# Latent attention of a two-layer trunk: TensorE held to program order, and a unit's transposes and value products regrouped into four steps

## The chip, the core and the metric

One core of one Trainium2 chip runs the whole program in one launch. The metric is the device time of that launch in microseconds, the median of several runs. TensorE (PE in the rows) does matrix products and transposes, VectorE (DVE), ScalarE (ACT) and GpSimd (POOL) do elementwise work, and SyncE (SP) issues the DMA transfers. PEld is TensorE's loading of weights, which runs beside its products.

## The reference, cut to what matters

The program computes two layers of a transformer trunk for 128 context tokens and 512 latent tokens. Each layer mixes a short convolution, differential attention with 4 heads and latent attention with 8 heads, and then a SwiGLU block. The change lies in the attention:

```python
def diff_block(qb):
    sc = jnp.einsum("bhmqd,bhmkd->bhmqk", qb, k_all).astype(jnp.float32) * DIFF_SCALE
    p = jax.nn.softmax(sc, axis=-1)
    a = p[:, :, 0] - lam * p[:, :, 1]
    return jnp.einsum("bhqk,bhkd->bhqd", a.astype(v_all.dtype), v_all)
...
def mla_block(qb):
    sc = jnp.einsum("bhqd,bhkd->bhqk", qb, k_m).astype(jnp.float32) * MLA_SCALE
    p = jax.nn.softmax(sc, axis=-1)
    return jnp.einsum("bhqk,bhkd->bhqd", p.astype(v_m.dtype), v_m)
```

Latent tokens attend to 640 keys (512 latent and 128 cached ones), context tokens to 128 keys.

## The kernel before

The attention of a layer is a list of numbered steps. A step is one *score*: the products of 128 queries with 640 keys for one head (`scores`, L1194, six matmuls for a latent head), the row maximum on VectorE (`nm`, L1198), the exponential with its sum on ScalarE (L1209), the reciprocal (L1247) and the scaling on GpSimd (L1248). Scores are written to PSUM tiles `mm`, of which there are two; `mm` is also used by a few other products (below).

Steps are grouped in *units*: a pair of heads and half of the 512 queries. Four units of differential attention have 8 steps each, eight units of latent attention 4 steps each, 64 steps in all. When a unit's scores are done, its value part follows (`av_steps`), in five parts, one for each block of 128 keys: four 128x128 transposes of the probabilities into a PSUM tile `trx` (L1269; there are two), a copy of it to an SBUF tile `PT` (the helper `copy`, L273 on ScalarE and L275 on VectorE, in turn), and two products with the values (L1280), which accumulate in the one tile `ac` and write 64 partitions each. Part kt transposes block kt + 1 and multiplies block kt. `LAG` says how many steps behind the unit's last score the parts begin.

Between the steps stand small jobs, each tied to a step number by `put`: the attention of the 128 context tokens, two parts for each pair of heads (`diff_prompt` and `mla_prompt`; the second part, `prompt_out`, transposes twice (L1316, L1317), copies, and multiplies with the values (L1322)); the norm of the differential heads (`diff_norm`: L1361, a chain of small VectorE operations, L1369); loads of queries and keys (`load_pair`) and of the context tokens' queries and keys (`p32`, tile name `p` in the rows); and, in layer 0 only, products of the next modulation vectors (`ada_pe`, L449 and L456). `SIDE`, `LOADS` and `ADA_N` hold their steps. The second parts, the norms and the modulation share one PSUM tile `tr`.

A scheduler that goes through the recorded program with durations of its own decides the order on every engine; instructions of neighbouring steps are interleaved where it finds an engine free. The first steps run beside the projections that make queries, keys and values. When these are recorded, the loop at the end of `attention` runs the rest, from about step 29 to the last value part. This text calls that stretch the *tail*: 240 to 353 us in layer 0 and 1097 to 1204 us in layer 1. Behind it stands the output projection (L349 with `w_out`).

Of the kernel before, what the change touches and what calls it, by code (L numbers as in the profile page):

```python
# [2 lines left out]

# [5 lines left out]
F32 = mybir.dt.float32  # L9
# [46 lines left out]
ADV = 0  # L56
HOLD = 2
LOADS = (29, 37, 43, 52)
SIDE = ((34, 37), (37, 40, 43), (36, 40), (47, 50, 56), (44, 47), (49, 51), (51, 54), (60, 62))
ADA_N = 12  # L60
ADA_IN = 1
ADA_PE = 6
# [2 lines left out]
ADA_FF2 = 1  # L65
ADA_LAG = 3
LAG = 4
STEPS = {"dv": (1, 2, 1, 1, 1), "ckv0": (0, 1), "ckv1": (0, 2), "ac1": (0, 2), "ab1": (0, 2), "cq0": (0, 2), "cq1": (0, 1), "dk1": (0, 0), "dq1": (0, 0)}
PAT = "PPPt"
PATC = "Pc"  # L70
# [128 lines left out]
class Trunk:  # L199
# [112 lines left out]
    def soon(self, n, fn):  # L312

        if n:
            self.defer(n, fn)
        else:
            fn()

    def tick(self):
        for x in self.later:  # L320
# [853 lines left out]
    def load_pair(self, p):  # L1174

        nc = self.nc
        for h in (2 * p, 2 * p + 1):
            k = [self.t(F32R, "mk") for _ in range(2)]
            q = [self.t(F32R, "mq") for _ in range(2)]
            for part in range(2):  # L1180
                r = slice(32 * h, 32 * h + 32)
                self.move(q[part][:96, :512], self.qd[r, :, part, :].rearrange("r i c -> (r i) c"))
                self.move(k[part][:96, :], self.kd[r, :, part, :].rearrange("r i c -> (r i) c"))
            self.mq[h], self.mk[h] = q, k
        self.p32[p] = self.at.tile([96, 2, 2, 128], F32, tag="p32", name="p32", bufs=2)
        nc.sync.dma_start(self.p32[p], self.pd[64 * p:64 * p + 64].rearrange("(h r) i a c -> (r i) h a c", h=2))

    def scores(self, pairs, qc):

# [21 lines left out]

    def pt(self):
        if self.at:
            return self.at.tile([128, 512], F32, tag="PT", name="PT", bufs=3)
        return self.t(name="PTt")[:, 0:512]

    def diff_unit(self, l, p, hf):
# [40 lines left out]
            self.ys[2 + p] = self.t(name="yo")  # L1258
        return self.ys[2 + p]

    def av_steps(self, tiles, v, dst, hf):
        nc = self.nc
        hold = {}

        def tp(kt):
            p = self.tr(True)
            for i in range(2):
                for q in range(2):
                    nc.tensor.transpose(p[:, 256 * i + 128 * q:256 * i + 128 * q + 128],  # L1269
                                        tiles[i, q][:, 128 * kt:128 * kt + 128], self.ident)  # L1270
            pt = self.pt()
            self.copy(pt, p)
            hold[kt] = pt

        def av(kt):
            if kt == 0:
                hold["acc"] = self.ac()
            acc = hold["acc"]
            for i in range(2):
                nc.tensor.matmul(acc[64 * i:64 * i + 64, :256], v(kt, i), hold[kt][:, 256 * i:256 * i + 256],  # L1280
                                 start=(kt == 0), stop=(kt == 4))
            if kt == 4:
                c0 = 384 * hf
                self.copy(dst[:, c0:c0 + 256], acc[:, :256])

        def step(kt):
            if kt == 0:
                tp(0)
            if kt < 4:
                tp(kt + 1)  # L1290
            av(kt)

        return [lambda kt=kt: step(kt) for kt in range(5)]

    def soft_prompt(self, ps, n, neg=None):
# [86 lines left out]
    def plan_steps(self, l):  # L1382
# [7 lines left out]
        def put(step, *fs):  # L1390
            self.after.setdefault(step, []).extend(fs)

        def parts(g, *at):
            state = []

            def step():
                if not state:
                    state.append(g())
                next(state[0], None)
            for i in at:  # L1400
                put(i, step)

        def unit(kind, p, hf, n):
            hold = {}
            g0 = len(self.steps)

            def start():
                hold["u"] = kind(l, p, hf)

            def step(i):  # L1410
                if i == 0:
                    start()
                hold["u"][0][i]()

            def av(kt):
                if kt == 0:
                    _, tiles, v, dst = hold["u"]
                    hold["av"] = self.av_steps(tiles, v, dst, hf)
                hold["av"][kt]()
            for i in range(n):  # L1420
                self.steps.append(lambda i=i: step(i))
            for kt in range(5):
                put(g0 + n - 1 + LAG + (n * kt) // 5, lambda kt=kt: av(kt))

        for kind, p, hf in units:
            unit(kind, p, hf, 8 if kind == self.diff_unit else 4)
# [1 line left out]
            put(i, lambda g=g: self.assemble_diff(1, 2 * g, 2 * g + 2))  # L1428
        for p, i in enumerate(LOADS):
            put(i, lambda p=p: self.load_pair(p))  # L1430
        parts(lambda: self.diff_prompt(l, 0), *SIDE[0])
        parts(lambda: self.diff_norm(l, 0), *SIDE[1])
        parts(lambda: self.diff_prompt(l, 1), *SIDE[2])
        parts(lambda: self.diff_norm(l, 1), *SIDE[3])
        for p in range(4):
# [15 lines left out]
    def attention(self, l):  # L1451
# [8 lines left out]
        for (kind, j), n in zip(JOBS, JSTEPS):  # L1460
            n = n if isinstance(n, tuple) else (0, n)
# [7 lines left out]
            self.tick()  # L1469
        self.W.lo_pool = False  # L1470
        self.stage("tr")
        while self.g < len(self.steps) or self.after:
            self.step(1)
        self.split_y(6)
        self.split_y(7)
        self.stage("any")
# [237 lines left out]
```

## Time and profile before

| what | value |
|---|---|
| median of 3 runs | 1756.45 us (1756.1 to 1757.79) |
| profiled execution, its own time | 1756.95 us |
| span of the profiled execution | 1755.2 us |
| TensorE busy | 1698.5 us, 97% of the span |
| VectorE, ScalarE, GpSimd busy | 56%, 35%, 14% |
| tail of layer 0 and of layer 1 | 113 us and 107.2 us |

The profiled execution's own time is 0.5 us above the median of the runs, and its span leaves out 1.75 us around it. A busy share is an average over stages; matmuls are pipelined, so that TensorE can be called busy while it streams less than it could.

### The profile page before, as it was taken

What the parts mean: (1) busy time and instruction counts of PE and PEld (TensorE: products, weight loads), DVE (VectorE), ACT (ScalarE), POOL (GpSimd) and SP (SyncE); (2) the same over time, 40 slices, a digit from 0 to 9 for tenths busy, and PEclk for the clock granted to TensorE, in tenths of its full rate; (3) what the DMA queues carried; (4) which work ended last, traced back from release to release, by engine and by line L of the source; (5) the groups of instructions that cost most, each with busy time, mean ns of one, the idle gap of its engine ahead of it and who ended that gap; (6) DMA issues with size and microseconds to landing.
All of it is one profiled execution on the core that took longest, in us unless ns stands there. A gap on an engine that the chain in (4) does not pass through costs nothing.

```text
span 1755.2 us, 29477 instructions
## 1 busy us (share of the span) xinstructions
PE 1698.5 (97%) x11983; PEld 1589.4 (91%) x11983; DVE 975.0 (56%) x1824; ACT 614.1 (35%) x1046; POOL 247.7 (14%) x226
## 2 busy tenths in 40 slices
PE   7999989999999999999999999899999999999997
PEld 6998867698999999999999997678999999999997
DVE  3656777747466656756476668774652233232236
ACT  1334555524432122122245546553353212212221
POOL 0011113440001010101211111332200000000014
PEclk9999989999999999999999999899999999999998
DMA  9665584321355545545314634622212222222211
GB/s 323 210 208 142 169 252 139 119 89 51 94 153 151 156 126 145 174 133 146 107 52 148 217 121 157 173 76 75 73 61 77 81 72 73 73 78 78 68 53 60
DMA packets 100871, 217.38 MB, mean 124 GB/s; under 512 B 12160, under 2 KB 28928, under 8 KB 100736
## 3 DMA queue, kind: packets, MB, share of 16 engines
q1 hardware_dynamic: 100736, 215.50, 39.7%
q8 instruction: 94, 1.54, 0.4%
q14 instruction: 41, 0.34, 0.1%
HBM read 185.28 MB, written 30.18 MB: 123 GB/s over the span
## 4 chain that ended last, share of the span: by engine, by line
PE 86%; DVE 5%; ACT 3%; DMA 2%; issue 2%; POOL 0%; SPq 0%; POOLq 0%; ACTq 0%; DVEq 0%
PE mm L349 61%; PE mm L1194 4%; PE mm L372 4%; PE ac L1280 3%; PE mm L1513 3%; PE trx L1269 3%; PE mm L994 2%; PE mm L401 1%; DMA rawt<-in_w_ada 1%; ACT hv L781 1%; PE ac L476 1%; ACT wu L138 1%; DVE wu L140 1%; PE tr L449 1%; DMA mk<-kd 1%
## 5 line engine op out<-in xcount | busy, mean ns | idle before, releaser
L349 PE MATMUL mm<-h,wu 128*128 128x384 f32 (+1 forms) x4944 | 734.6, 309 | 1.8 <-ACT kp L908 1.5
L349 PEld LDWEIGHTS mm<-h,wu 128*128 128x128 f32 x4944 | 723.3, 188 | 8.7 <-issue 5.3
L138 ACT CAST wu<-stg 128x1024 fp32r<-128x1024 f32 (+2 forms) x200 | 201.5, 1011 | 686.1 <-PE mm L349 333.0
L140 DVE TENSOR_TENSOR wu<-stg,wu 128x1024 fp32r<-128x1024 f32 (+2 forms) x200 | 239.3, 1199 | 155.9 <-ACT wu L138 153.6
L349 PE MATMUL mm<-gh,wu 128*128 128x256 f32 (+1 forms) x1184 | 258.6, 309 | 0.0
L349 PEld LDWEIGHTS mm<-gh,wu 128*128 128x128 f32 x1184 | 198.7, 188 | 0.9 <-issue 0.6
L349 PE MATMUL mm<-gl,wu 128*128 128x384 f32 (+1 forms) x592 | 182.8, 309 | 0.0
L1198 DVE TENSOR_REDUCE nm<-mm 128x1 f32<-128x640 f32 x128 | 104.7, 818 | 50.4 <-PE mm L1194 49.6
L1547 DVE TENSOR_TENSOR gs<-gs,mm 128x640 f32<-128x640 f32 (+2 forms) x48 | 36.6, 763 | 154.2 <-PE mm L349 149.4
L668 DVE SCALAR_TENSOR_TENSOR x<-mm,ga,x 128x512 f32<-128x512 f32 x48 | 35.9, 749 | 145.6 <-PE mm L349 145.6
L349 PEld LDWEIGHTS mm<-gl,wu 128*128 128x128 f32 x592 | 111.4, 188 | 0.2 <-issue 0.2
L527 DVE SCALAR_TENSOR_TENSOR acc<-rawt,scT,acc 128x512 f32<-128x512 f32 x98 | 74.7, 763 | 60.4 <-DMA rawt<-in_w_ada 59.0
L372 PE MATMUL mm<-h,wu 128*128 128x384 f32 (+1 forms) x576 | 99.5, 331 | 7.4 <-ACT h L782 7.1
L372 PEld LDWEIGHTS mm<-h,wu 128*128 128x128 f32 x576 | 92.2, 205 | 12.6 <-ACT h L782 10.2
L349 PE MATMUL mm<-hi,wu 128*128 128x384 f32 (+1 forms) x400 | 89.9, 311 | 0.1
L687 POOL TENSOR_TENSOR accS<-x 128x640 f32<-128x640 f32 x4 | 9.9, 2488 | 507.3 <-DVE x L674 494.7
L1194 PE MATMUL mm<-mk,mq 96*128 96x384 f32 (+1 forms) x384 | 75.0, 336 | 5.2 <-ACT P L1209 2.4
L532 DVE SCALAR_TENSOR_TENSOR rawt<-rawt,scT 128x512 f32<-128x512 f32 x98 | 74.7, 762 | 2.1 <-POOL rawt L525 2.1
L1194 PEld LDWEIGHTS mm<-mk,mq 96*128 96x128 f32 x384 | 63.7, 200 | 12.3 <-ACT P L1209 5.2
L349 PEld LDWEIGHTS mm<-hi,wu 128*128 128x128 f32 x400 | 68.0, 188 | 2.6 <-issue 1.5
L1209 ACT ACTIVATE P<-mm,nm 128x640 f32<-128x640 f32 x56 | 44.6, 797 | 55.7 <-DVE nm L1198 45.0
L525 POOL TENSOR_SCALAR acc<-rawt,scT 128x512 f32<-128x512 f32 x14 | 9.8, 697 | 376.2 <-PE tr L542 376.1
(272 smaller groups left out, 2251.8 us busy)
## 6 DMA issues: line engine op xcount, KB each, us to landing
stg<-in_w_ff SPq DMA_DIRECT2D x104, 512.0 KB, 3.6
rawt<-in_w_ada SPq DMA_DIRECT2D x160, 256.0 KB, 3.1
stg<-in_w_in SPq DMA_DIRECT2D x30, 512.0 KB, 4.4
stg<-in_w_ff SPq DMA_DIRECT2D x32, 448.0 KB, 3.3
raw<-in_w_ada SPq DMA_DIRECT2D x32, 256.0 KB, 6.2
stg<-in_w_out SPq DMA_DIRECT2D x16, 512.0 KB, 4.4
mk<-kd SPq DMA_DIRECT2D x32, 240.0 KB, 5.8
mq<-qd SPq DMA_DIRECT2D x32, 192.0 KB, 5.4
```

What stands on the lines that cost most here:

```text
L138: nc.scalar.copy(u[:, 0, :ncol], t[:, :ncol])
L140: (nc.gpsimd if self.lo_pool else nc.vector).tensor_sub(u[:, 1, :ncol], t[:, :ncol], u[:, 0, :ncol].bitcast(F32))
L349: self.last = nc.tensor.matmul(out, w(k, pw), x(k, px), start=(k == 0 and i == 0), stop=(k == nk - 1 and i == 2)).ins
L372: self.last = nc.tensor.matmul(ps, u[:, pw, 128 * k:128 * k + 128], x(k, px)[:, c0:c1], start=(k == 0 and i == 0), stop=(k == NK - 1 and i ...
L527: nc.vector.scalar_tensor_tensor(self.acc[0], w, c[0], self.acc[0], ALU.mult, ALU.add)
L532: nc.vector.scalar_tensor_tensor(self.acc[1], w, c[1], self.acc[1], ALU.mult, ALU.add)
L1194: nc.tensor.matmul(ps[:, 128 + c0:128 + c1], q[:96, qc:qc + 128], k[:96, c0:c1], start=(i == 0), stop=(i == len(pairs) - 1))
L1198: nc.vector.tensor_reduce(nm, s, axis=AX.X, op=ALU.max, negate=True)
L1209: self.exp_end = nc.scalar.activation(P, s, AF.Exp, bias=nm, accum_out=sm).ins
L1269: nc.tensor.transpose(p[:, 256 * i + 128 * q:256 * i + 128 * q + 128], tiles[i, q][:, 128 * kt:128 * kt + 128], self.ident)
L1280: nc.tensor.matmul(acc[64 * i:64 * i + 64, :256], v(kt, i), hold[kt][:, 256 * i:256 * i + 256], start=(kt == 0), stop=(kt == 4))
L1513: self.last = self.nc.tensor.matmul(ps[:, c0:c1], u[:, pw, 128 * k:128 * k + 128], x(k, px)[:, c0:c1], start=(k == 0 and j == 0), stop=(k ...
```

## The change

Inside the tail every TensorE instruction is tied to the one recorded before it (`in_order`), so that the scheduler keeps TensorE's program order there. For the units that begin at step 24 or later (one unit of differential attention and the eight of latent attention) the value part has four parts in place of five: the transposes of blocks 0 and 1, of block 2, of blocks 3 and 4, and then all ten value products. They stand 3, 4, 5 and 6 steps behind the unit's last score. `PT` has six buffers for three, `p32` one for two; `p32` is loaded at steps of its own; and two context jobs stand some steps later.

```diff
-SIDE = ((34, 37), (37, 40, 43), (36, 40), (47, 50, 56), (44, 47), (49, 51), (51, 54), (60, 62))
+SIDE = ((34, 37), (37, 40, 43), (38, 41), (47, 50, 56), (44, 47), (49, 51), (54, 56), (60, 62))
+LAGM = 3
+NPT = 6
+P32 = (38, 45, 50, 56)
...
+    @contextmanager
+    def in_order(self):
+
+        traced, prev = self.nc.cur_bb.bb.instructions, self.pe_end
+        n = len(traced)
+        yield
+        for i in traced[n:]:
+            if i.engine == self.nc.tensor.engine:
+                if prev is not None:
+                    self.tc.add_manual_dep(i, prev.name, mybir.DependencyInfo(mybir.DependencyClass.NoSync,
+                                                                              mybir.DependencyReason.DATA))
+                prev = i
+        self.pe_end = prev
...
-        self.p32[p] = self.at.tile([96, 2, 2, 128], F32, tag="p32", name="p32", bufs=2)
-        nc.sync.dma_start(self.p32[p], self.pd[64 * p:64 * p + 64].rearrange("(h r) i a c -> (r i) h a c", h=2))
+
+    def load_p32(self, p):
+
+        self.p32[p] = self.at.tile([96, 2, 2, 128], F32, tag="p32", name="p32", bufs=1)
+        self.nc.sync.dma_start(self.p32[p], self.pd[64 * p:64 * p + 64].rearrange("(h r) i a c -> (r i) h a c", h=2))
...
-            return self.at.tile([128, 512], F32, tag="PT", name="PT", bufs=3)
+            return self.at.tile([128, 512], F32, tag="PT", name="PT", bufs=NPT)
...
+        if batch:
+            return [lambda kts=kts: [tp(kt) for kt in kts] for kts in ((0, 1), (2,), (3, 4))] + \
+                [lambda: [av(kt) for kt in range(5)]]
         return [lambda kt=kt: step(kt) for kt in range(5)]
...
+            batch = g0 >= 24
...
-            for kt in range(5):
-                put(g0 + n - 1 + LAG + (n * kt) // 5, lambda kt=kt: av(kt))
+            for kt in range(4 if batch else 5):
+                put(g0 + n - 1 + (LAGM + kt if batch else LAG + (n * kt) // 5), lambda kt=kt: av(kt))
...
+        for p, i in enumerate(P32):
+            put(i, lambda p=p: self.load_p32(p))
...
+        self.pe_end = None
         while self.g < len(self.steps) or self.after:
-            self.step(1)
+            with self.in_order():
+                self.step(1)
```

Three places show what the change makes of the engines' orders. The lines of the changed kernel are numbered anew: the scores are L1214 (before: L1194), the transposes L1291 (L1269), the value products L1302 (L1280), `prompt_out` L1341, L1342 and L1347 (L1316, L1317 and L1322), the context scores of latent heads L1371 (L1346).

First, TensorE in layer 1, in the middle of the tail. Before, the value products of each block stand by themselves between transposes and scores:

```order
L1194 MATMUL mm<-mk,mq 128x384 x3
L1194 MATMUL mm<-mk,mq 128x256 x3
L1280 MATMUL ac<-PT,vm 64x256 x2
L1269 MATMUL trx<-first,P 128x128 x2
L1269 MATMUL trx<-first,Pc 128x128 x2
L1346 MATMUL mm<-p_11931 128x128 x2
L1280 MATMUL ac<-PT,vm 64x256 x2
```

In the changed kernel the ten products of a unit stand in one row, behind a score:

```order
L1291 MATMUL trx<-first,P 128x128 x2
L1291 MATMUL trx<-first,Pc 128x128 x2
L1214 MATMUL mm<-mk,mq 128x384 x3
L1214 MATMUL mm<-mk,mq 128x256 x3
L1302 MATMUL ac<-PT,vm 64x256 x10
L1371 MATMUL mm<-p_12247 128x128 x2
L1214 MATMUL mm<-mk,mq 128x384 x3
```

Counted over the tails, runs of instructions that write 64 or 32 partitions (value products, L1322, L1369, and in layer 0 L449) go from 55 to 29 in layer 0 and from 42 to 18 in layer 1.

Second, TensorE at a `prompt_out` in layer 1. Before, other work stands between its transposes and its products:

```order
L1316 MATMUL tr<-first,PT 128x128
L1317 MATMUL tr<-first,PT 128x128
L1346 MATMUL mm<-p_12174 128x128 x2
L1280 MATMUL ac<-PT,vm 64x256 x2
L1269 MATMUL trx<-first,P 128x128 x2
L1269 MATMUL trx<-first,Pc 128x128 x2
L1322 MATMUL tr<-PT,vmp 64x128 x2
```

Now the products follow the transposes directly, and the copy that feeds them (VectorE or ScalarE) has nothing beside it on TensorE. This is so at six places in each layer:

```order
L1291 MATMUL trx<-first,P 128x128 x2
L1291 MATMUL trx<-first,Pc 128x128 x2
L1341 MATMUL tr<-first,PT 128x128
L1342 MATMUL tr<-first,PT 128x128
L1347 MATMUL tr<-PT,vmp 64x128 x2
L1214 MATMUL mm<-mk,mq 128x384 x3
```

In layer 0 the transpose of a modulation vector (L473 of the changed kernel) likewise stands directly behind the products that it takes (L466) at three places, and L466 directly behind the norm's products in the same tile `tr` (L1386) at two.

Third, VectorE in layer 1 at the second `diff_prompt`, whose product on TensorE (L1332, now L1357) takes a tile that VectorE multiplies first (L1329, now L1354). Before, the multiplication stands one score ahead of the operation that reads the product (L1300):

```order
L1309 TENSOR_SCALAR psm_11821<-psm_11821,neglam_491 128x2
L1329 TENSOR_TENSOR PT_11886<-kp32_9536,first_97 128x512
L1247 RECIPROCAL r0_11842<-sm_11840 128x1
L1198 TENSOR_REDUCE nm_11869<-mm_11862 128x1
L1336 TENSOR_TENSOR PT_11823<-PT_11823 128x2x128
L1300 TENSOR_REDUCE pm_11890<-mm_11888 128x4
```

Now it stands behind the copy of the step's second block of transposes, and so it is at all four `diff_prompt` of the program:

```order
L1218 TENSOR_REDUCE nm_11954<-mm_11947 128x1
L278 COPY PT_11974<-trx_11969 128x512
L1354 TENSOR_TENSOR PT_11978<-kp32_9536,first_97 128x512
L1267 RECIPROCAL r0_11959<-sm_11957 128x1
L1325 TENSOR_REDUCE pm_11982<-mm_11980 128x4
```

On TensorE the product that takes `PT_11978` stands directly behind the transposes into `trx_11969`.

## Rows read from the trace of the kernel before

**Rows 1.** The page: busy time by engine, and the chain that ended last.

```profile
PE 1698.5 (97%) x11983; PEld 1589.4 (91%) x11983; DVE 975.0 (56%) x1824; ACT 614.1 (35%) x1046; POOL 247.7 (14%) x226
...
PE 86%; DVE 5%; ACT 3%; DMA 2%; issue 2%; POOL 0%; SPq 0%; POOLq 0%; ACTq 0%; DVEq 0%
```

**Rows 2.** Busy time in stretches of both tails (columns in the first line).

```profile
core 0: us, PE busy (x) PEld busy (x) DVE busy (x) ACT busy (x) POOL busy (x), PEclk, DMA share, GB/s
258.00:342.00 84.00, 82.08 (x692) 59.84 (x691) 62.81 (x155) 43.16 (x95) 33.39 (x38) 1.00 0.48 139
...
1101.00:1111.00 10.00, 7.25 (x25) 6.19 (x26) 6.53 (x14) 4.75 (x10) 1.60 (x2) 0.51 1.02 317
...
1115.00:1193.00 78.00, 75.72 (x558) 56.36 (x558) 55.21 (x133) 42.16 (x94) 30.93 (x36) 1.00 0.31 87
```

**Rows 3.** TensorE's waits (total, times, longest), layers 0 and 1; two by time.

```profile
PE mm L1194 <- ACT P L1209: 4.6, 3, 2.5
...
PE tr L1316 <- DVE ada_acc L512: 0.8, 1, 0.8
PE tr L1316 <- DVE mod L457: 0.8, 1, 0.8
...
PE mm L1194 <- ACT P L1209: 5.9, 4, 1.9
...
PE mm L1194 <- DVE r L1247: 0.9, 1, 0.9
...
242.06 0.56 PE L1194 MATMUL mm<-dkp,dqp 96*128 96x384 f32 x2 [1.89 <-ACT P L1209]
...
1102.19 0.90 PE L1194 MATMUL mm<-dkp,dqp 96*128 96x384 f32 x2 [1.83 <-ACT P L1209]
```

**Rows 4.** TensorE by time at the end of layer 1's tail (start, length).

```profile
1194.32 0.65 PE L1280 MATMUL ac<-PT,vm 128*64 128x256 f32 x4
1194.90 0.44 PE L1269 MATMUL trx<-first,P 128*128 128x128 f32 x2
...
1195.49 0.65 PE L1280 MATMUL ac<-PT,vm 128*64 128x256 f32 x4
...
1199.02 0.44 PE L1269 MATMUL trx<-first,P 128*128 128x128 f32 x2
...
1200.04 1.08 PE L1280 MATMUL ac<-PT,vm 128*64 128x256 f32 x8
1201.05 0.44 PE L1269 MATMUL trx<-first,P 128*128 128x128 f32 x2
```

**Rows 5.** All engines by time: a score, and the score that waits for its tile.

```profile
1141.96 1.13 PE L1194 MATMUL mm<-mk,mq 96*128 96x384 f32 x6
...
1142.93 0.27 PE L1269 MATMUL trx<-first,P 128*128 128x128 f32 x1
...
1143.18 0.82 DVE L1198 TENSOR_REDUCE nm<-mm 128x1 f32<-128x640 f32 x1 [0.74 <-PE mm L1194]
...
1144.10 0.79 ACT L1209 ACTIVATE P<-mm,nm 128x640 f32<-128x640 f32 x1 [4.28 <-DVE nm L1198]
...
1145.04 1.14 PE L1194 MATMUL mm<-mk,mq 96*128 96x384 f32 x6 [1.17 <-ACT P L1209]
```

**Rows 6.** Durations on VectorE and ScalarE (min/median/max ns, or by time), and a load's landing.

```profile
L273 ACT COPY PT<-trx x54: 574/586/598, 256.0 to 1202.9; 128x512 f32<-128x512 f32 x54
L275 DVE COPY PT<-trx x36: 671/683/694, 257.4 to 1201.8; 128x512 f32<-128x512 f32 x36
...
313.22 0.42 DVE L275 COPY PT<-tr 128x256 f32<-128x256 f32 x1 [0.59 <-PE tr L1317]
...
L1329 DVE TENSOR_TENSOR PT<-kp,first x4: 680/849/1098, 234.3 to 1117.3; 128x512 f32<-128x512 f32 x4
...
312.35 0.28 DVE L512 TENSOR_TENSOR ada_acc<-tr,ada_acc 128x128 f32<-128x128 f32 x1
...
DMA to landing us min/median/max: 2.5/3.5/6.9
```

More of the change, by code (lines that the diff above doesn't have):

```diff
@@ L1 @@
 import math
-from contextlib import ExitStack, nullcontext
+from contextlib import ExitStack, contextmanager, nullcontext
 import numpy as np
@@ L1259, in ob, with av_steps @@
         return self.ys[2 + p]
-    def av_steps(self, tiles, v, dst, hf):
+    def av_steps(self, tiles, v, dst, hf, batch):
         nc = self.nc
@@ L1417, in av @@
                     _, tiles, v, dst = hold["u"]
-                    hold["av"] = self.av_steps(tiles, v, dst, hf)
+                    hold["av"] = self.av_steps(tiles, v, dst, hf, batch)
                 hold["av"][kt]()
```

## The prediction

> **What bounds the kernel now.** I read the page first, then the busy times of the two tails, TensorE's waits there, and its instructions by time. The page shows TensorE busy for 97% of the span, and 86% of the chain that ended last is its own work [rows 1]. In the tails it is the same: 82.1 of 84 us and 75.7 of 78 us in their long middles, while VectorE is busy for 75% and 71% of them [rows 2]. The waits outside the first 10 us of each tail are few. In layer 0 three waits for the exponential sum to 4.6 us, of which 1.89 and 2.5 lie at the start, and two for the shared tile `tr` cost 0.8 each; in layer 1 the four sum to 5.9, of which 1.9 and 1.83 lie at the start, and one of 0.9 stands beside them [rows 3]. That leaves 1.8 + 3.1 = 4.9 us of waits in both. So the old order has TensorE streaming nearly all the time, and a gain must come out of the stream itself.
>
> There is something to gain in it. Products of one block go from 1194.32 to 1194.90 and four transposes from there to 1195.49, so 0.58 and 0.59 us. Eight transposes in one go take 1.02 (1199.02 to 1200.04), 0.16 less than twice 0.59, and the products of two blocks in one go 1.01, 0.15 less than twice 0.58 [rows 4]. So each change to products that write 64 partitions and back costs 0.30 us beside the products.
>
> **The change, part by part.**
>
> *Regrouping.* The order shows 26 such visits fewer in layer 0 and 24 in layer 1: 50 x 0.30 = **-15.0 us**, all on the engine that sets the pace. If part of it hides in waits it is less; -12.5 is my bound (0.25 each). The number of products, transposes and scores stays. The Trainium skill says the same of the cause ("TensorEngine Tiling (Array Packing)", Key Properties): changing the tiling mode, not merely the tile, drains the engine; by that rule only the number of changes counts, and the sum stays -15.0. The rows agree, since a visit with twice the products pays the 0.15 once.
>
> *Program order at `prompt_out`.* Two transposes, a copy on VectorE or ScalarE, and products that need it now stand in one row, 12 times. The bare chain is 0.25 us to the engine that copies (a score's last matmul gives way at 1142.93, its VectorE reader starts at 1143.18), 0.42 for the copy, and 0.15 back (the exponential ends at 1144.89, TensorE starts at 1145.04) [rows 5, 6]: 0.82, less some 0.15 of the change of layout, which then hides: 0.65 at least. But the copy also queues behind the same step's score. Counted from that score's last matmul, the maximum runs from 0.25 to 1.07; a copy behind it ends at 1.49 and the products start at 1.64, while TensorE, with four transposes (0.44) and two more, is free at 0.66: 1.0 us. Behind ten products it is 0.75, since TensorE comes later; where the norm's VectorE work, or exponential and another copy, stand ahead of it I work out 1.4 to 1.8. Mean 1.1 less the hidden 0.1: 12 x 1.0 = **+12.0 us** (bounds 7.8 and 21.6, at 0.65 and 1.8).
>
> *Program order at `diff_prompt`.* VectorE's multiplication now stands behind the copy of the second block of transposes, and TensorE's product directly behind those transposes, four times. From the end of the transposes: 0.25, the copy 0.68, the multiplication 0.68 to 1.10, 0.15 back [rows 5, 6], so 1.75 to 2.2; I take 1.8, the lower part, because a wait for the tile `mm` (next) is partly under it: **+7.2 us** (6.8 to 8.8).
>
> *The two `mm` tiles.* A score can be written when the exponential two tiles back has been read. That chain is 2.11 us (1142.93 to 1145.04 [rows 5]). Where a context product takes the other tile after eight transposes, TensorE is back after some 1.4 us (0.11 for each transpose, and as much for each of the four passes of the context products, with a little between), so it waits 0.7; I count six such places, and two of about 0.5 at the norms, less one that the modulation fills: 4.5. They replace the 4.9 us of waits above: **-0.4 us** (bounds -4.9, if these vanish, and +4, if the other engines run later than I think).
>
> *Layer 0's modulation.* Three transposes behind their own products: 0.25 + 0.28 + 0.15 [rows 5, 6], 0.7 each. Two product groups wait until a small VectorE operation, no longer than that 0.28, has read `tr`: 0.6 each. **+3.3 us** (2 to 5).
>
> *The end of each tail.* The last unit's 20 transposes stand in one row, with two tiles: a tile is back after 0.25 + 0.59 to 0.68 + 0.15, about 1.0 us, and the other tile's four transposes fill 0.44. Three such waits of 0.55 in each tail are 3.3; the old end has its own, of which these rows say nothing: I take the middle, **+1.5 us** (0 to 3.3).
>
> *Costed at nothing.* `PT` with six buffers takes no instruction. `p32` with one buffer must wait for the product before it, but four steps lie between load and use, each with a score of 0.97 and its share of the rest, over 2 us; a load lands within 6.9 us [rows 5, 6]. Uncovered it would cost at most that, and SP's loads of later heads behind it have as many steps. The start of the tails (10 us each, at a granted clock of about half in most of it [rows 2]) has nearly the same order as before: 0, within 2 us either way.
>
> One rule speaks against the change. The Trainium skill ("TensorE: Matmul & The Clock Gate", Part 2, Step-by-step) says that matmuls stay in program order and only weight loads are pulled ahead, so that a score behind a waiting product doesn't pass it. No row here shows one that passed; could it pass, the sum would lose 12.0, 7.2 and 3.3.
>
> **Sum.** -15.0 + 12.0 + 7.2 - 0.4 + 3.3 + 1.5 = +8.6 us. The profiled execution took 1756.95, so 1765.5 for such a one; it lies 0.5 above the median, so **1765.0 us**. About 0.2%, 3.5 us, is what a measurement of this kernel can tell from no change.
>
> **Rivals.**
>
> *Faster: the waits stand in for others.* The 16 waits at the context jobs cost 19.2 us in my sum; the rest is -10.6. While TensorE waits there, VectorE and ScalarE catch up, and the scores that follow find their tiles free. If a place costs net less than 0.44 us, the kernel is faster by over 0.2%; at 0.15 it is -8.2, 1748 us. For it: VectorE and ScalarE have a quarter of the middle and more to spare [rows 2]. Against: only 4.9 us of old waits are there to be replaced. Chance 0.26.
>
> *No change.* The same places cost 0.44 to 0.88 each, near the bare chain: copies seldom queue. 1753 to 1760 us, about 1757. Against it stands the order, in which the copies follow the maximum or the exponential of their step. Chance 0.20.
>
> *The clock falls in the tails.* At the start of layer 1's tail, after waits of 1.9 and 1.83 us close together, the granted clock is 0.51 for 10 us, the lower of the levels 1.2 and 2.4 GHz; in the middles it is 1.00 [rows 2, 3]. The new waits are as long at `diff_prompt` and at the worst copies. Ten us of streaming at half the clock would cost up to 5 us more in each layer: +8.6 + 10 = 1775 us. Against it: new waits are mostly single, and the waits of 0.8 to 1.17 in the old middles left the clock at 1.00. Chance 0.10. The Trainium skill has a rule to this ("Perfetto Trace Analysis", Matmul Optimizations): the engine scales power with utilization, so matmuls should run back to back in batches. The stretch at 0.51 agrees.
>
> *The regrouping saves nothing.* If the 0.30 us were the copies' lateness and not the change of layout, the waits would come without the gain: +23.6, 1780 us. Against it: the 0.15 is the same wherever I look. Chance 0.03.
>
> **How the numbers follow.** My forecast, +3.5 to +14 us (1760 to 1771), has the remaining 0.41. Slower by over 0.2%: 0.41 + 0.10 + 0.03 = 0.54; within 0.2%: 0.20; faster: 0.26. The range of 1748 to 1777 leaves out the lower half of the faster case and most of what lies beyond the clock's.
>
> **What would show it.** In the changed profile ten products of a unit should take 5 x 0.43 + 0.3, about 2.4 us in one row, against 2.9 before. Each L1347 should stand 0.65 to 1.8 us behind L1342, with a copy from `tr` as the releaser; L1357 should wait some 1.8 us for VectorE; and scores behind L1371 some 0.7 us for the exponential. The middles would then show TensorE's busy share below today's 97%, at a granted clock of 1.00. The forecast fails if the waits at the 16 places sum to less than 10 us, or if those tails' other engines run late enough to add waits at ordinary scores, of which I counted none.

## The result, and the profile after

The changed kernel takes 1777.6 us (median of 4 runs, 1772.8 to 1783.7), the kernel before 1757.1 beside it: 1.011 times as long, interval 1.0093 to 1.0126. It is slower, as forecast, but by more than twice the forecast, and 0.6 us beyond the end of the range. Eleven more runs of it (below) lie between 1773.8 and 1780.3; the median of all 15 is 1775.8, that of 76 runs of the kernel before, taken beside the experiments, 1757.7.

The page of the changed kernel, busy time by engine and the chain that ended last:

```profile
PE 1691.5 (96%) x11983; PEld 1595.9 (90%) x11983; DVE 981.6 (55%) x1824; ACT 615.0 (35%) x1046; POOL 245.3 (14%) x226
...
PE 80%; DVE 8%; ACT 5%; DMA 4%; issue 3%; SPq 1%; POOL 0%; POOLq 0%; ACTq 0%; DVEq 0%
```

TensorE does the same number of instructions as before [rows 1], and the chain that ended last now goes through VectorE and ScalarE for 13% where it was 8%. Busy time in the stretches of both tails:

```profile
core 0: us, PE busy (x) PEld busy (x) DVE busy (x) ACT busy (x) POOL busy (x), PEclk, DMA share, GB/s
...
258.00:352.00 94.00, 80.47 (x707) 64.33 (x708) 66.41 (x158) 44.48 (x97) 31.66 (x38) 0.98 0.44 127
...
1111.00:1125.00 14.00, 10.34 (x34) 7.60 (x34) 8.68 (x19) 7.00 (x15) 2.40 (x3) 0.51 1.02 300
1125.00:1212.00 87.00, 73.68 (x565) 59.95 (x566) 61.41 (x139) 45.10 (x100) 30.54 (x37) 1.00 0.29 84
```

In the middles TensorE is busy for 86% and 85%, where it was 98% and 97% [rows 2]: it now waits. In layer 1 the stretch at the granted clock of 0.51 is 14 us long, where 10 us were shown before. Below, a tail runs from the last product of the projections ahead of it to the first product of the output projection behind it; so measured the two are 115.2 and 106.7 us long before and 124.8 and 114.5 us now. The idle time that TensorE's rows show in them (every gap over 0.15 us) sums to 16.4 us before and 39.6 us now. The waits of TensorE in the tails, layer 0 and then layer 1:

```profile
PE mm L1214 <- ACT P L1229: 5.5, 3, 1.9
PE mm L1357 <- DVE r L1267: 2.9, 2, 1.5
PE tr L1347 <- DVE PT L278: 2.7, 3, 1.1
PE tr L1347 <- ACT PT L276: 2.2, 3, 1.1
PE tr L473 <- DVE ada_acc L529: 1.9, 3, 0.9
PE mm L1214 <- DVE PT L1328: 1.1, 1, 1.1
...
PE mm L1214 <- ACT P L1229: 5.4, 4, 1.9
PE tr L1347 <- DVE PT L278: 3.1, 3, 1.4
PE mm L1357 <- DVE r L1267: 2.9, 2, 1.5
PE tr L1347 <- ACT PT L276: 2.2, 3, 1.1
...
PE mm L1214 <- DVE PT L1328: 1.4, 2, 1.1
```

The prediction named these places: `prompt_out` (L1347), `diff_prompt` (L1357), the modulation (L473) and the scores (L1214) behind context scores. Of the 5.5 and 5.4 us at L1214, though, 3.7 are two waits at the start of each tail, which the kernel before has too [rows 3]; the rest are single scores behind context scores, 1.8 in layer 0 and 1.1 and 0.6 in layer 1. What a wait at the first two looks like, by time, one place each:

```profile
299.13 0.27 PE L1342 MATMUL tr<-first,PT 128*128 128x128 f32 x1
...
299.59 0.41 DVE L278 COPY PT<-tr 128x256 f32<-128x256 f32 x1
...
300.06 0.44 PE L1347 MATMUL tr<-PT,vmp 128*64 128x128 f32 x4 [0.66 <-DVE PT L278]
```

```profile
254.67 0.69 DVE L278 COPY PT<-trx 128x512 f32<-128x512 f32 x1 [0.88 <-PE trx L1291]
...
255.28 0.68 DVE L1354 TENSOR_TENSOR PT<-kp,first 128x512 f32<-128x512 f32 x1
255.88 0.15 DVE L1267 RECIPROCAL r<-sm 128x1 f32<-128x1 f32 x1
...
256.11 0.67 PE L1357 MATMUL mm<-PT,qp 128*128 128x512 f32 x1 [1.48 <-DVE r L1267]
```

In the second the row names the reciprocal as releaser, but the operand is written by the multiplication L1354, which ends at 255.96; the product starts 0.15 later. Both places have the form that the prediction gave them; in the first pattern the wait is longest, 1.5 us, where other work of VectorE stands ahead of the copy.

A single wait is counted here as in the prediction, from the point at which TensorE could go on. For a transpose that is 0.11 us after its start, some 0.16 us earlier than the end that its row has: the wait at 300.06 above is 0.82 by this count and 0.66 by the row. Sums over a tail are the rows' own idle time.

Ten products of a unit in one row:

```profile
318.26 2.38 PE L1302 MATMUL ac<-PT,vm 128*64 128x256 f32 x20
320.56 0.45 PE L1214 MATMUL mm<-mk,mq 96*128 96x384 f32 x1
```

That is 2.30 us from their start to the next score, where the kernel before needed five times 0.58 [rows 4].

### The profile page after: what moved, and what is told of

Its sections match the earlier page's. It is cut to its first block, busy times and chain, and to the rows that moved or that the text cites. A ratio compares the mean times of both kernels' runs of the same rounds, so it can differ in the third digit from the quotient of the medians.

```text
span 1771.0 us, 29478 instructions
## 1 busy us (share of the span) xinstructions
PE 1691.5 (96%) x11983; PEld 1595.9 (90%) x11983; DVE 981.6 (55%) x1824; ACT 615.0 (35%) x1046; POOL 245.3 (14%) x226
## 3 DMA queue, kind: packets, MB, share of 16 engines
q8 instruction: 94, 1.54, 0.4%
## 4 chain that ended last, share of the span: by engine, by line
PE 80%; DVE 8%; ACT 5%; DMA 4%; issue 3%; SPq 1%; POOL 0%; POOLq 0%; ACTq 0%; DVEq 0%
PE mm L366 60%; PE mm L1214 4%; PE mm L389 3%; PE mm L1543 3%; PE ac L1302 2%; PE mm L418 2%; PE trx L1291 1%; ACT hv L798 1%; DVE nm L1218 1%; PE mm L1011 1%; PE ac L493 1%; DMA stg<-in_w_in 1%; DMA mk<-kd 1%; ACT PT L276 1%; ACT wu L141 1%
## 5 line engine op out<-in xcount | busy, mean ns | idle before, releaser
L1214 PE MATMUL mm<-mk,mq 96*128 96x384 f32 (+1 forms) x384 | 80.4, 346 | 9.0 <-ACT P L1229 3.5
L1214 PEld LDWEIGHTS mm<-mk,mq 96*128 96x128 f32 x384 | 65.7, 203 | 22.7 <-issue 11.4
L366 PE MATMUL mm<-lo,wu 128*128 128x384 f32 (+1 forms) x200 | 61.8, 309 | 0.0
```

Source lines behind the costliest of these rows:

```text
L366: self.last = nc.tensor.matmul(out, w(k, pw), x(k, px), start=(k == 0 and i == 0), stop=(k == nk - 1 and i == 2)).ins
L1214: nc.tensor.matmul(ps[:, 128 + c0:128 + c1], q[:96, qc:qc + 128], k[:96, c0:c1], start=(i == 0), stop=(i == len(pairs) - 1))
```

## The experiments

Two figures of a run help to compare kernels that differ by a few microseconds: its time, and the mean granted clock of its span (1 is full speed). Within one kernel the runs with the lower mean clock are the longer ones. Over 175 runs of the 14 kernels, each kernel taken about its own mean, 0.001 less of mean clock goes with 1.5 us more. The last column moves a kernel's mean time along this slope to a mean clock of 0.984, that of the kernel before. This is a correlation, not a cause shown. The error of a mean so moved is 0.2 to 0.9 us, so that two rows of the table differ by more than the noise only where they are some 2 us apart.

| kernel | median us (runs) | times before (95%) | mean clock | us at 0.984 |
|---|---|---|---|---|
| before | 1757.7 (76) | | 0.984 | 1758.7 |
| changed (three times) | 1775.8 (15) | 1.011, 1.010, 1.011 | 0.980 | 1771.9 |
| e1_free | 1758.3 (10) | 1.0007 (0.9997 to 1.0016) | 0.984 | 1758.2 |
| e3_out | 1771.3 (10) | 1.0071 (1.0053 to 1.0089) | 0.980 | 1766.2 |
| e4_km | 1767.6 (10) | 1.0046 (1.0020 to 1.0071) | 0.982 | 1765.3 |
| e5_waits | 1764.5 (5) | 1.0049 (1.0031 to 1.0067) | 0.979 | 1758.1 |
| e6_ring | 1783.0 (4) | 1.0148 (1.0133 to 1.0163) | 0.978 | 1774.4 |
| e7_all | 1756.3 (10) | 0.9992 (0.9983 to 1.0002) | 0.983 | 1754.9 |
| e8_visits | 1779.7 (4) | 1.0105 (1.0061 to 1.0149) | 0.981 | 1775.2 |
| e9_split | 1756.1 (10) | 0.9988 (0.9967 to 1.0010) | 0.981 | 1753.1 |
| e10_fill | 1798.2 (4) | 1.0211 (1.0177 to 1.0245) | 0.982 | 1794.4 |
| e11_late | 1748.5 (6) | 0.9939 (0.9916 to 0.9962) | 0.984 | 1748.7 |
| e12_fill | 1776.1 (6) | 1.0094 (1.0076 to 1.0112) | 0.982 | 1770.7 |
| e13_split | 1776.6 (5) | 1.0110 (1.0089 to 1.0130) | 0.980 | 1770.3 |

**Without the binding.**

```diff
-            with self.in_order():
-                self.step(1)
+            self.step(1)
```

> The change without the binding of TensorE to program order; the four-part value work, the buffers and the moved jobs stay. If the loss comes from TensorE waiting where program order puts a dependent product directly behind what it needs, the scheduler fills those places again: 1750 to 1760 us, about as fast as before (its order has 53 and 37 visits to 64 or 32 partitions, 55 and 42 before, which is worth 2 us). If the loss comes from the regrouping itself (value work later, six PT buffers, one p32 buffer), it stays above 1768 us.

1758.3 us, no different from the kernel before. The scheduler takes the regrouped value parts apart again: in the rows of the two tails TensorE goes to products that write 64 or 32 partitions 51 and 37 times, where the kernel before does 51 and 42 times by the same count and the changed one 29 and 18. So the loss comes with the binding, and so does the gain in visits. (The opposite, binding without regrouping, wasn't tried; I expect the old value parts of two neighbouring units to wait for each other there over the one tile `ac`.)

**The waits at the context jobs.** e3_out puts the products of `prompt_out` a step behind their transposes, e4_km the multiplication of `diff_prompt` a step ahead of its product, and e5_waits does both and, inside the tail, puts the end of a modulation vector a step later (last pair of lines). `SIDE` gets the extra steps:

```diff
 self.copy(pt[:, :256], p[:, :256])
-acc = p[:, 256:384]
+yield
+acc = self.tr()[:, 256:384]
...
 nc.vector.tensor_mul(kv, ...)
+yield
 ps = self.mm()
...
-self.ada_finish(self.ada_part, key)
+self.after.setdefault(self.g + 1, []).append(lambda acc=self.ada_part: self.ada_finish(acc, key))
```

> The changed kernel with the products of prompt_out one step behind their transposes and copy (12 places). Theory (the 12.2 us of waits there are net cost): the waits go, of which 2 to 3 us come back as waits for the shared tile tr, so 9 to 10 us less than the changed kernel, near 1768 where the changed kernel has 1777. Rival (a wait there lets the other engines catch up, so that it replaces others): waits at the scores behind the context jobs grow by most of it, and the time stays within 3 us of the changed kernel's.

> The changed kernel with diff_prompt's multiplication one step ahead of its product (4 places). Theory (the 6.8 us of waits there are net cost): TensorE has no wait at that product, 6 to 7 us less than the changed kernel, near 1771 where the changed kernel has 1777. Rival (part of the wait hides a wait for the tile mm behind it): 3 to 4 us come back as waits of the scores behind that product, so near 1774.

> The change, with the dependent work a step later: prompt_out's products one step behind its transposes, diff_prompt's multiplication one step ahead of its product, the modulation's transpose one step behind its products. The profile of the change shows 12.2 us, 6.9 us and 2.7 us of waits there. If these waits are lost time, 1756 to 1766 us; if they only stand in for waits that TensorE would have anyway (the two mm tiles), less than 5 us comes back, 1770 us or more.

e4_km: the theory holds. No wait at the product is left, and the time at equal clock is 6.6 us less than the changed kernel's, for waits of 6.8 (by the plain medians 8.2 us less). e3_out lies between theory and rival: 12.2 us of waits go (10.2 by the rows), 5.7 come off at equal clock. Its waits in layer 0 show where some of the rest went:

```profile
PE mm L1214 <- ACT P L1229: 6.4, 5, 1.9
PE tr L473 <- DVE ada_acc L529: 1.9, 3, 0.9
PE mm L1214 <- DVE PT L1328: 1.6, 1, 1.6
PE mm L1358 <- DVE r L1267: 1.5, 1, 1.5
PE mm L1358 <- DVE PT L1355: 0.9, 1, 0.9
PE tr L466 <- ACT yo L276: 0.8, 2, 0.4
```

The scores wait 8.0 where it was 6.6, and the modulation now waits for the copy out of `tr` (L466, twice by this row). In both tails the rows' waits fall from 39.6 to 31.2 us, by less than the 10.2 taken away. So a wait at `prompt_out` did stand in for others, by about half if one goes by time and by less if one goes by the rows. All three edits together (e5_waits) bring 13.8 us at equal clock, and the rows' waits are 25.1.

**The tiles of the context scores.** e6_ring writes the scores of `diff_prompt` and `mla_prompt` into `tr`, so that they leave the two `mm` tiles to the others; e7_all does this on top of e5_waits, e9_split does it in layer 1 alone, and e11_late in layer 0 too for the last two latent pairs, the third of the four pairs a step later, behind the modulation. The lines are e11_late's; e6_ring has `self.tr()` without a condition:

```diff
-ps = self.mm()
+ps = self.tr() if l or p >= 2 else self.mm()
...
-... (54, 56, 57), (60, 62, 63))
+... (55, 57, 58), (60, 62, 63))
```

> The change, with the context tokens' scores written to the tile tr in place of an mm tile, so that the latent scores alternate between two mm tiles undisturbed. The profile of the change shows about 8 us of waits of scores behind L1371 and some 1.5 us behind L1357. If the mm tiles are the part of the loss that the prediction priced too low, 1763 to 1771 us; if those waits come from late VectorE and ScalarE in general, within 3 us of the change.

> Both repairs together: dependent work a step later, and context scores in tr. If regrouping saves what its fewer changes of layout promise (about 10 us by the profile of the change, 15 by the prediction) and the waits are the whole loss, this is faster than the kernel before: 1744 to 1754 us. If it ends at 1757 us or above, the regrouped order has costs of its own.

> All three waits taken away as in e7_all, but the context scores take the tile tr in layer 1 alone, and mm in layer 0, where the modulation's products use tr as well. Theory (places add up, and each tail is what it was in the run that had it best): tails of 116.9 and 101.6 us as profiled, against 122.5 and 101.6 in e7_all, so 5.6 less than e7_all's 1756.3: 1751 us, and faster than the kernel before by 0.3%. Rival (the tails' length is set by time at the lower granted clock, which comes and goes with the order): 1756 or more, with low-clock time in layer 0's tail as in e7_all.

> e9_split with two places of layer 0 moved: the context scores of the last two latent pairs take tr there too, and those of the third pair stand a step later, behind the last modulation products. e9_split shows waits of 2.65 and 1.73 us at the scores behind these two places, and 5 of 0.5 to 0.7 at the modulation that stay. Theory: these 4 us go from layer 0's tail (117.1 to about 113.5) and nothing comes in their place, so 3 to 4 us below e9_split's 1756: 1752 to 1753, faster than the kernel before by 0.3%. Rival (time at the lower clock eats it, as it did with e7_all's 5.5 us): span times mean clock falls from 1722.5 to 1719, but the time stays at 1755 or above.

e6_ring was a miss: slower still. In layer 0 `tr` now makes the modulation wait, in three rows of its waits there:

```profile
PE tr L466 <- issue: 2.6, 2, 1.6
...
PE tr L466 <- DVE dv L1388: 1.8, 2, 1.5
PE tr L466 <- DVE PT L1328: 1.6, 1, 1.6
```

In layer 1, without modulation, the scores' waits behind context scores went from 3.3 us to 0.4, and its tail from 114.5 us to 112.4, with 20.5 us at the lower clock in it where the changed kernel's trace has 13.7. e7_all, with e5_waits under it, is as fast as the kernel before; its tail of layer 1 is 101.6 us long, that of layer 0 still 122.5. e9_split takes the good half: its profiled tails are 117.1 and 102.0 us long, as the theory had it (116.9 and 101.6), yet its median equals e7_all's, at a mean clock of 0.981 against 0.983; the rival was right about the time. At equal clock it is 1.8 better, not 5.6. The two profiled runs show where it went: their mean clocks are the same (0.982), the tails are 5.0 us shorter in sum, but the span only 1.4. Outside the tails the lower clock was granted for 20.4 us, in e7_all's run for 13.6. e11_late is as the theory had it and a little better, 1748.5 us, faster than both kernels; the rival falls. Its middles:

```profile
256.00:345.00 89.00, 83.34 (x747) 66.74 (x741) 67.16 (x165) 47.21 (x102) 33.55 (x40) 0.98 0.51 151
...
1112.00:1190.00 78.00, 75.11 (x596) 61.96 (x594) 60.87 (x143) 47.97 (x103) 31.56 (x38) 1.00 0.33 99
```

TensorE is busy for 94% and 96% there, and its tails are 114.1 and 101.9 us long, where the changed kernel's are 124.8 and 114.5.

**Why the scores wait longer than counted.** Two places of layer 1 of the changed kernel, by time. The first is the plain case, a latent score whose tile the next score needs (ScalarE and TensorE; the score's last matmul gives way at 1155.38):

```profile
1156.52 0.58 ACT L276 COPY PT<-trx 128x512 f32<-128x512 f32 x1 [2.17 <-PE trx L1291]
1157.00 0.80 ACT L1229 ACTIVATE P<-mm,nm 128x640 f32<-128x640 f32 x1
...
1156.26 0.61 PE L1371 MATMUL mm<-p 96*128 96x128 f32 x4
1157.94 0.61 PE L1214 MATMUL mm<-mk,mq 96*128 96x384 f32 x2 [1.07 <-ACT P L1229]
```

The copy of the second four transposes stands ahead of the exponential on ScalarE, and the chain from score to score is 2.56 us long (1155.38 to 1157.94), not 2.11 [rows 5]; TensorE is back at 1156.70, about where I had put it, and waits 1.24. The other case, VectorE and then TensorE:

```profile
1198.36 2.16 DVE L854 TENSOR_TENSOR lo<-y,hi 128x640 fp32r<-128x640 f32 x1
1200.44 0.68 DVE L278 COPY PT<-trx 128x512 f32<-128x512 f32 x1
...
1201.11 0.80 DVE L1218 TENSOR_REDUCE nm<-mm 128x1 f32<-128x640 f32 x1
...
1201.17 0.44 PE L1291 MATMUL trx<-first,P 128*128 128x128 f32 x2 [0.56 <-DVE PT L278]
...
1202.94 0.71 PE L1371 MATMUL mm<-p 96*128 96x128 f32 x4 [0.68 <-ACT Pc L1229]
1204.74 0.41 PE L1214 MATMUL mm<-mk,mq 96*128 96x384 f32 x1 [1.09 <-DVE PT L1328]
```

A split of a residual tile (L854) takes 2.16 us, and TensorE then waits three times, 0.7, 0.8 and 1.25. Layer 0 has the same at 339 to 345 us. e13_split moves this split to step 62:

```diff
-for i, j in enumerate((58, 59, 56, 57, 58, 62)):
+for i, j in enumerate((58, 62, 56, 57, 58, 62)):
```

> The changed kernel with one of VectorE's splits of a residual tile (y1) three steps later, at step 62. In the changed kernel it stands beside GpSimd's split of another tile and takes 2.15 us in both layers, where the same operation by itself takes 0.81; behind it the row maximum of a score, its exponential and a copy of transposes are late, and TensorE waits three times close together (0.7, 0.84 and 1.25 us, 2.8 in each layer). Theory (the two-tile term was too small because VectorE was late there): with the split gone from that place the first two waits vanish and the third falls to about 0.7, so waits of 2.1 us go in each layer, 4 us in all at the same mean clock, and the split takes 0.8 us where it now stands. Rival (the waits are those of the row itself, whatever VectorE does): all three stay within 0.3 us of what they are, and the time stays within 1.5 us of the changed kernel's at the same clock.

Half of it came: the waits of 0.7 and 0.8 are gone in both layers, so these were VectorE's lateness. The third did not fall to 0.7 but rose to 1.58 in both, and the split's new place brought a wait at the last value products:

```profile
1210.28 1.12 PE L1214 MATMUL mm<-mk,mq 96*128 96x384 f32 x6 [1.42 <-DVE PT L1328]
...
1222.96 0.65 PE L1302 MATMUL ac<-PT,vm 128*64 128x256 f32 x4 [0.78 <-ACT PT L276]
```

That second wait is 0.21 by the row in the changed kernel. In both tails together the rows' waits fall by only 1.3 us, and at equal clock 1.6 came off, not 4, a difference that the noise alone could make. The long wait behind a context score belongs to the row itself, as the rival had it for all three: ahead of the operations that read the context product, VectorE has a copy and a row maximum, which end at 1209.34.

**Visits.** e8_visits does the ten products of a unit in three visits, behind the transposes of later blocks:

```diff
+def tp_av(a, b):
+    for kt in a: tp(kt)
+    for kt in b: av(kt)
...
+return [lambda: tp_av((0, 1), ()), lambda: tp_av((2,), (0,)), lambda: tp_av((3, 4), (1, 2)), lambda: tp_av((), (3, 4))]
```

> The changed kernel with the ten products of a unit in three visits between its transposes and not in one, bound to program order as before: 28 more visits in both tails (43 and 32 against 29 and 18 in the trace's rows). Theory (a visit costs 0.30 us of TensorE's own time): 8.4 us more, less what of it lies in waits that shorten: 1781 to 1785 where the changed kernel has 1776, and the unexplained rest of the tails (10 and 6 us outside waits) grows by 7 to 8.5 in all. Rival (the 0.30 is lateness of the copies, which one visit merely moves): the rest of the tails does not grow by more than 3 us, and the time stays within 3 us of the changed kernel's.

1779.7 us, 3.9 above the median of the changed kernel's runs, 3.3 at equal clock: the sign is the theory's, the size is under half of 8.4. But the theory allowed for waits that shorten, and they did: the rows' waits in the tails are 36.4 us, 3.2 less than in the changed kernel. So 28 visits cost some 6.5 us of other time, 0.23 each, an estimate that the noise alone leaves open by 0.07. e11_late gives another: it is 10.0 us faster than the kernel before at equal clock with 3.6 us more of the rows' waits (20.0 against 16.4) and 49 visits fewer in its tails, which makes 0.28 a visit. Both are near the rows' 0.30.

**The clock.** The changed kernel was run twice more, and twice with TensorE kept busy in waits, by products of an operand with itself that nothing reads:

```diff
+for _ in range(14):    # e10_fill; 7 in e12_fill
+    nc.tensor.matmul(ps[:, 512:640], self.qp32[:, p, :], self.qp32[:, p, :], start=True, stop=True)
 nc.tensor.matmul(ps[:, :512], self.qp32[:, p, :], km, start=True, stop=True)
...
+for _ in range(5):    # e10_fill alone
+    nc.tensor.matmul(p[:, 384:512], self.ident, self.ident, start=True, stop=True)
```

> The changed kernel once more, for its spread. My account of its profiled execution gives waits of 39.0 us in both tails where the kernel before has 7.6, a gain of about 15 us on visits of products, and a tail total of +18.7; the executions before this one lay between 1772.8 and 1783.65 us with mean granted clocks of 0.984 down to 0.978. Theory (waits are fixed by the order, and the rest of the spread is time at the lower granted clock): times between 1772 and 1784, and in this order of the mean clock, higher time with lower clock. Rival (the waits themselves vary): the same mean clock goes with times several us apart, and this profile's sum of waits differs from 39.0 by more than 4.

> The changed kernel with TensorE kept at work in the waits: 5 products of the identity with itself (about 0.11 us each, into an unused part of the tile) ahead of each of the 12 waiting pairs of prompt_out, and 14 such products ahead of each of the 4 waiting products of diff_prompt; nothing reads them. They fill 0.55 of about 1.0 us and 1.5 of 1.7 us. By span times mean granted clock, the changed kernel is 12 us above the one before (1740 and 1728), and the other 7 us are time at the lower clock (34.7 against 27.5 us lost). Theory (idle time in the waits brings the lower clock): span times clock stays near 1740, the mean clock rises from 0.980 to 0.984 or more, and the time falls to 1768 to 1771. Rival (the clock has nothing to do with these waits): the mean clock stays at 0.980 to 0.981, and the time at 1775 or, where a filling is longer than its wait, above.

> The changed kernel beside e12_fill: 1772 to 1784 us, span times mean clock 1740, mean clock 0.980.

> The changed kernel with only the 4 waits of diff_prompt filled: 7 products of an operand with itself, two passes of 0.11 us each, so 1.55 us, stand ahead of the waiting product, whose wait is 1.64 to 1.79 us; nothing reads them. (In e10_fill the fillings were twice as long as meant, and those of prompt_out stood behind the wait for the copy and not in it.) Theory (idle time at these four places, which lie in the first 20 us of each tail, holds the clock down): span times mean clock stays at 1740, the loss to the lower clock falls from 34.7 to the 31.6 us of e4_km, which has no wait there, and the time by 3 us against the changed kernel run beside it. Rival (the clock doesn't hang on these waits, and e4_km gained only by its order): both stay the same, within 1.5 us.

The waits of the changed kernel repeat (39.6 us by the rows in the first trace, 37.9 in the second, 39.0 in the third), so its spread is not in them; it goes with the clock. But span times clock isn't constant, as I had it: 0.001 of mean clock would then go with 1.8 us, and it goes with 1.5. That a slower clock costs nothing while TensorE waits would explain it, but no run shows it. In the third trace the lower clock in layer 1 is not confined to the start:

```profile
1111.00:1132.00 21.00, 16.48 (x56) 12.77 (x56) 12.44 (x23) 8.83 (x19) 3.20 (x4) 0.51 1.04 290
1132.00:1218.00 86.00, 74.11 (x542) 59.91 (x542) 57.76 (x132) 42.63 (x94) 29.26 (x36) 0.94 0.20 61
```

e10_fill tells nothing of the clock: such a product is two passes of 0.11 us, so that the fillings were twice too long, and those of `prompt_out` themselves waited for the copy (4.9 us in layer 0 by the rows, as much as the changed kernel at L1347). e12_fill fills the four waits of `diff_prompt` as meant, and these are gone from its trace; its mean clock is 0.9817 beside 0.9808 of the changed kernel in the same comparison, and its median 1.9 us lower. That lies between theory and rival, with two of its six runs at 1769 and 1770 us and four at 1776 to 1777. Whether the waits bring the lower clock stays open. That it comes with the binding of this order (0.980 against 0.984 without it) is shown, and also that e11_late, with 20.0 us of waits, is back at 0.984. Against the waits as the cause speaks that e5_waits, with 25.1 us of them, has 0.979, and e4_km, with 33.6, has 0.982.

## Why the prediction fell short

The direction held, the size didn't: +8.6 us were predicted, and +18.9 measured between the means of all runs (15 and 76), 13.2 of them at equal clock. By the prediction's own steps:

*Regrouping, -15.0.* Right: 2.30 us for ten products (2.4 forecast), and 46 visits fewer by the tails' rows, 50 by the order shown ahead of the prediction. With the waits that the runs above could take away gone, the changed order is 10.0 us below the kernel before at equal clock (e11_late), and the price of a visit that this and e8_visits give (0.28 and 0.23) is near the 0.30 of the sum. The Trainium skill ("TensorEngine Tiling (Array Packing)", Key Properties) says that a change of tiling mode drains TensorE. The sign of both runs agrees.

*`prompt_out`, +12.0.* Twelve waits of 0.68 to 1.54 us, 12.2 in all. Their size was right and their price wasn't: only 5.7 us came off when they were taken away (e3_out), as some of them replaced other waits. That is what the rival for "faster" said of all of them.

*`diff_prompt`, +7.2.* Four waits of 1.64 to 1.79 us, 6.8 in all, and 6.6 at equal clock when they are taken away: right.

*The two `mm` tiles, -0.4.* This step failed. I had put 4.5 us of new waits for six places and two norms, and they are 10.7: 6.5 at five scores behind latent context scores (0.8 to 1.98 each where I had 0.7) and 4.2 at others near them. I had taken the bare chain of [rows 5], and left out that ScalarE copies transposes ahead of the exponential (0.45 us more, in the plain case), that VectorE has a copy and a row maximum ahead of the readers of a context product, and that VectorE may be in a long operation (0.7 + 0.8 in each layer, gone in e13_split). The 4.9 us of old waits that I set against them were misread too, to the other side: outside the first 10 us of each tail the kernel before has about 7 us by the rows, as I had left out one of 1.2 us for a DMA and the small ones. From e5_waits to e11_late, whose edits touch little else, 9.4 us came off at equal clock; the rows' waits fall by 5.1 between them, and where the rest comes from is not shown.

*Layer 0's modulation, +3.3; the end of the tails, +1.5.* The modulation's waits are 3.7. At the ends the rows show 1.8 us of waits where the old ends have 0.65, so +1.2. Both are right.

*The clock, a rival at 0.10.* It came in part. The profiled run of the changed kernel had nearly the mean clock of the kernel before (0.984 and 0.985), but the mean over 15 runs is 0.9805, worth 5.7 us by the slope. It was no step of the sum, and I had looked for it in one profiled execution, where it hardly shows. That the rival's 1775 us is near the measured time is luck: it rests on the sum of 8.6, which was too low, and on 10 us for the clock, which were too many.

So of the 10.3 us between 8.6 and 18.9 the slope puts 5.7 on the clock, and 4.6 are missing in the sum. With the measured waits in place of the forecast ones the sum is -15.0 + 12.2 + 6.8 + 10.7 - 4.9 + 3.7 + 1.2 = +14.7: the two tiles alone add 6.2 to the forecast, and the other terms nearly cancel. With 7 us of old waits in place of 4.9 it is 12.6. The 13.2 at equal clock lie between. By time the runs share it out otherwise (5.7 for `prompt_out`, 9.4 from e5_waits to e11_late), because a wait that is taken away at one place partly comes back at the next score, so that the order of the edits decides which of them gets the credit. Of the rivals, "no change" and "regrouping saves nothing" fall; "faster" becomes true only when the waits are taken away.

## What to carry to other kernels

An engine held to program order is worth what one takes out of its row: put each product a step behind the copy or multiplication that feeds it, and let a product that is read late take another tile than the two that the next products need, where that other tile is free (in layer 1 `tr` was; in layer 0 the modulation then waited for it). Here the same binding is 1% slower than the free order without this care and 0.6% faster with it. When a wait for a tile is estimated, count on each engine what stands ahead of the reader, copies above all, and not the bare chain alone. And compare the mean clock of several runs before a few microseconds are put down to an order.

## What the runs showed of the hardware that was not expected

VectorE's split of a residual tile, a subtraction of two SBUF tiles, takes 0.81 us by itself, and 2.16 in layer 1, where GpSimd has begun its own split 0.11 us earlier (at 1198.25, 1.58 us long). The four splits of this kind in the changed kernel, two in each layer, with durations in ns (min/median/max):

```profile
L854 DVE TENSOR_TENSOR lo<-y,hi x4: 812/1481/2158, 337.0 to 1198.4; 128x640 fp32r<-128x640 f32 x4
```

With the one moved (e13_split) all four take 814 or 815. The 2.16 is GpSimd's remaining 1.47 us and then 0.69. The Trainium skill ("SBUF — State Buffer", SBUF: two separate sides) says that VectorE with two SBUF inputs and GpSimd share a port pair as an exclusive lock, held for the whole instruction; these rows agree.

Mean granted clocks from 0.979 to 0.985 occurred in runs of one and the same kernel (e4_km, 1763.6 to 1774.4 us), so that a single run of it is good to 0.6% only.
